# Seven products in place of eight in the up projections of a two-layer transformer kernel

## The chip, the cores and the metric

The kernel runs on one core of one Trainium2 chip. The metric is device time per execution in microseconds (us), the median of several runs, lower is better. Engines are called PE (matmul), DVE (vector), ACT (scalar), POOL and SP; here SP only issues DMAs.

## The reference

256 tokens of width 2048 pass two layers, each an attention mixer and an MLP. The change is in the MLP alone:

```python
h = rms_norm(x, norm_mlp[i])
x = x + jnp.square(jax.nn.relu(h @ w_up[i])) @ w_down[i]
```

`w_up[i]` is 2048 x 8192, `w_down[i]` 8192 x 2048, all in fp32.

## The kernel before

A weight matrix is worked through in **items**: 256 rows by 512 columns (512 KB). For each item a raw fp32 block is loaded by SP (`load`, L978), ACT rounds it to `wh` (L995) and DVE forms the rest `wl` (L996). PE multiplies high by high, low by high and high by low: 2 token halves x 2 row blocks x 3 = 12 matmuls of 128x512, `wh` first, `wl` in the last third (`high_first`). The items stand in one list. At item i the program splits item i+2 (`LEAD`) and loads item i+7 (five raw buffers, three pairs of `wh`, `wl`), runs item i's matmuls, then its `post` steps, then the steps that `later` set due. Instructions under `keep` hold this order on their engine; the sections on both sides of the MLPs are ordered by a scheduler.

The MLP goes in four slices f of 2048 hidden columns, in the order up(0), up(1), down(0), up(2), down(1), up(3), down(2), down(3). **Up** before: four chunks c of 512 columns, each of 8 items, summed in PSUM (`acc`). `up_done` hands a finished chunk to `to_features`: DVE transposes 32x32 blocks (L167), SP writes four pieces to DRAM (`td`, L173) an item later and reads them back (L179) four items after that, and `relu2` (DVE, L348), `high` (ACT, L353) and `low` (DVE, L358) make the two parts of `hT`, the left operand of down.

**Down** before takes two column blocks of 512 at once (`down_pair`). Of the 8 row blocks two (`SEVEN = (0, 2)`) and the two token halves form a 2x2 by 2x2 block product, which the scheme of Strassen in Winograd's form does with seven half items of 6 matmuls instead of four items of 12. The other six row blocks are plain. One pair is the order

```python
TURNS = "G0 H0 s1 G1 s3 H1 G2 s6 H2 s5 G3 s7 H3 s2 G4 H4 s4 G5 H5".split()
```

G and H are the plain items of the two columns, s1 to s7 the products. `s5`, `s6`, `s7` have no load: they split sums of weight blocks that DVE makes (`t1` to `t4`, L464 to L473, into X, Z, Y). Their left operands are sums of token blocks, made by `sums` into `S`. Products s1, s5, s6, s7 land in `aux` PSUM and are gathered in `E` by `p1` (ACT, L477), `p6`, `p5`, `p7` (DVE, L480 to L487); `into` (L494) and `add_residual` (L310) add the results to the residual.

Of the kernel before, what the change touches and what calls it, by code (L numbers as in the profile page):

```python
# [17 lines left out]
P = 128  # L18
# [43 lines left out]
def trunk(ctx, tc, x, x_t, gains_t, w_in_a, w_out_a, w_in_b, w_out_b, rel_bias, w_up, w_down, out):  # L62
# [23 lines left out]
    def copy(o, i, scale=1.0):  # L86
        pin(act.activation(o, i, AF.Copy, scale=scale))
# [67 lines left out]
    def later(n, f, *a):  # L155

        due[clock[0] + n].append(lambda: f(*a))

    def to_features(parts, place, then, wait=0):


        n = sum(part.shape[1] // P for part in parts)
        y = tmp.tile([P, 8, P], F32, name="jx", bufs=3)[:, :n, :]
        m = 0
        for part in parts:
            k = part.shape[1] // P
            dve.transpose(y[:, m:m + k, :].rearrange("p k f -> p (k f)"), part)  # L167
            m += k
        d = drp.tile([4, 32, n, 4, 32], F32, name=f"td{n}", bufs=4)

        def write():
            for a in range(4):
                keep(nc.sync.dma_start(d[:, :, :, a, :].rearrange("b j n i -> j n b i"),  # L173
                                       y[32 * a:32 * a + 32].rearrange("p n (b i) -> p n b i", b=4)))
            later(4, read)

        def read():
            z = place()
            keep(nc.sync.dma_start(z, d.rearrange("b j n a i -> (b j) n (a i)")))  # L179
# [148 lines left out]
    def mlp(l, next_col):  # L328
# [2 lines left out]

        def begin(pl):
            sec["pool"] = pl

        def stats():
# [4 lines left out]
        def up_done(f, c, acc):  # L340
            def parts(z):
                hT = sec[f][:, 4 * c:4 * c + 4].rearrange("p k i (t q) -> p i t k q", t=2)
                return z.rearrange("p (t k) q -> p t k q", t=2), hT[:, 0], hT[:, 1]

            def relu2(z):
                if c == 0:
                    sec[f] = sec["pool"].tile([P, KT, 2, S], F32R, name="hT", bufs=2)
                keep(dve.scalar_tensor_tensor(z, z, 0.0, z, op0=OP.max, op1=OP.mult))  # L348
                later(1, high, z)

            def high(z):
                r, h, l = parts(z)
                keep(act.activation(h, r, AF.Copy))  # L353
                later(1, low, z)
# [5 lines left out]
            to_features(acc, any_tile, relu2)  # L360

        def down_done(f, g, acc):
            if f < 3 or next_col is not None:
# [24 lines left out]
        def sums(f):  # L388

            h = sec[f]  # L390
            a, b = any_tile(), any_tile()
            a = a.rearrange("p (q j t) e -> p q j (t e)", q=2, j=KB)
            hi, lo = (h[:, 0:2 * STEP, i, :].rearrange("p (q j) s -> p q j s", q=2)[:, :, :KB]
                      for i in range(2))
            dve.tensor_add(a, hi.bitcast(F32), lo.bitcast(F32))
            b4 = b.rearrange("p (s j) e -> p s j e", s=4)
            (a11, a21), (a12, a22) = ((a[:, q, :, :P], a[:, q, :, P:]) for q in range(2))
            dve.tensor_add(b4[:, 0], a21, a22)
            dve.tensor_sub(b4[:, 1], b4[:, 0], a11)
            dve.tensor_sub(b4[:, 2], a11, a21)  # L400
            dve.tensor_sub(b4[:, 3], a12, b4[:, 1])
            z = sec["S"] = sec["pool"].tile([P, 2, 4 * KB, P], F32R, name="S", bufs=1)
            copy(z[:, 0], b)
            dve.tensor_sub(z[:, 1], b, z[:, 0].bitcast(F32))

        def down_pair(f, n):


            base = len(items)
            keys = [("dn", 2 * n + i) for i in range(2)]  # L410
            qs = [q for q in range(QB) if q not in SEVEN]

            def plain(col, i):
                def mm(wh, wl):
                    if i == 0:
                        acc = accp.tile([P, 2, 512], F32, name="acc")
                        accs[keys[col]] = [acc[:, t, :] for t in range(2)]
                    acc, L = accs[keys[col]], sec[f]
                    for t, j, part, wx, a, z in high_first(wh, wl):
                        keep(pe.matmul(acc[t], L[:, KB * qs[i] + j, part, t * P:(t + 1) * P],  # L420
                                       wx[:, j, :], start=a and i == 0,
                                       stop=z and i == len(qs) - 1))
                it = Item(rows(w_down[l], 2048 * f + KB * P * qs[i], KB * P,
                               1024 * n + 512 * col, 512), KB, 512, mm)
                if i == len(qs) - 1:
                    it.post.append(lambda: down_done(f, 2 * n + col, accs.pop(keys[col])))
                return it

            def seventh(left, src, to=None):


                def mm(wh, wl):
                    if to is None:
                        p = auxp.tile([P, 512], F32, name="aux")
                    else:
                        p = accs[keys[to[0]]][to[1]]
                    for t, j, part, wx, a, z in high_first(wh, wl, 1):
                        keep(pe.matmul(p, left(part, j), wx[:, j, :], start=to is None and a,  # L438
                                       stop=to is None and z))
                    it.product = p  # L440
                own_rows = not isinstance(src, str)
                it = Item(src if own_rows else None, KB, 512, mm)
                if not own_rows:
                    it.form = lambda: sec[src]
                return it

            def own(q, t):
                return lambda part, j: sec[f][:, KB * q + j, part, t * P:(t + 1) * P]

            def summed(i):  # L450
                return lambda part, j: sec["S"][:, part, KB * i + j, :]

            def block(col, q):
# [12 lines left out]
            def t2():
                keep(dve.tensor_sub(new("Z"), seven["s3"].raw, sec["X"]))

            def t3():
                keep(dve.tensor_sub(sec["Y"], seven["s3"].raw, sec["Y"]))  # L470
# [2 lines left out]
                keep(dve.tensor_sub(sec["Z"], seven["s2"].raw, sec["Z"]))  # L473

            def p1():
                sec["E"] = sec["pool"].tile([P, 4, 512], F32, name="E", bufs=1)
                keep(act.activation(sec["E"][:, 0], seven["s1"].product, AF.Copy))  # L477

            def p6():
# [9 lines left out]
                                    sec["E"][:, 1:3]))  # L489

            def into(t):
                xc = xs[:, t, 1024 * n:1024 * n + 1024].rearrange("p (c e) -> p c e", c=2)
                E = sec["E"].rearrange("p (c t) e -> p c t e", t=2)[:, :, t]
                keep(dve.scalar_tensor_tensor(xc, E, sec["rs2"][:, t:t + 1], xc,  # L494
                                              op0=OP.mult, op1=OP.add))

            qa, qb = SEVEN
            seven = {
# [11 lines left out]
            items[base - 8].early.append(load_y)  # L510
            for name, step in (("H0", t1), ("s1", p1), ("G1", t2), ("H1", t3), ("H2", p6), ("G3", p5),
                               ("H3", t4), ("G4", p7), ("H4", lambda: into(0)),
                               ("G5", lambda: into(1))):
                items[base + TURNS.index(name)].post.insert(0, step)

        def down(f):
            tail = next_col is None and f == 3
# [17 lines left out]
        items[10].post.append(stats)  # L535
        return items, begin


# [523 lines left out]
```

## Time and profile before

| | us |
|---|---|
| median of 3 runs (2063.6 to 2066.08) | 2064.94 |
| the profiled execution | 2063.33 |
| its span in the profile | 2061.5 |
| PE busy / DVE busy / ACT busy | 2053.8 / 1453.9 / 1025.4 |

The profile is of one execution; the chain that ended last runs through PE alone but for shares that round to nothing. PE's busy time counts 390 ns for a matmul that overlaps its neighbours, so the pace is read from the start times of the timeline.

### The profile page before, as it was taken

The page shows a single profiled execution, that of the slowest core. Times are in us where ns is not written, and L with a number is a line of the kernel's source. Part 1 is how long each engine was busy: PE and PEld are TensorE (multiplying, and loading weights), DVE is VectorE, ACT ScalarE, POOL GpSimd, SP SyncE. Part 2 cuts the span into 40 slices and gives each one's busy share as a digit, 9 for nine tenths or more (in the row PEclk, how much of TensorE's full clock was granted, in tenths as well). Part 3 has the DMA queues.
Part 4 walks back from the last instruction along what each step waited for, and adds up shares of the span by engine and source line. Part 5 has one row for each costly group of instructions (what it writes and reads, how often), then busy time and mean ns, then how long its engine had stood idle before and what let it go on. Part 6 is the DMA issues. An engine that isn't in the chain of part 4 may idle for free. (4 is left out here: it accounts for less than half of the span.)

```text
span 2061.5 us, 24939 instructions
## 1 busy us (share of the span) xinstructions
PE 2053.8 (100%) x9164; PEld 1697.1 (82%) x9164; DVE 1453.9 (71%) x1581; ACT 1025.4 (50%) x1233; POOL 28.9 (1%) x71
## 2 busy tenths in 40 slices
PE   9999999999999999999999999999999999999999
PEld 7888888888888888888887788888888888888887
DVE  5555655666687687678885798675668767867885
ACT  6555554544454454455554566454445445444543
POOL 0110100000000000000000000000000000000000
PEclk9999999999999999999999999999999999999999
DMA  9888856888866876876688688498886678678664
GB/s 315 236 228 213 237 173 202 264 240 247 238 220 184 246 242 194 234 229 213 192 253 251 195 251 259 150 255 245 247 257 213 196 234 243 192 211 259 205 196 164
DMA packets 477467, 464.85 MB, mean 225 GB/s; under 512 B 269664, under 2 KB 279968, under 8 KB 477344
## 3 DMA queue, kind: packets, MB, share of 16 engines
q1 hardware_dynamic: 469488, 455.81, 74.1%
q10 hardware_dynamic: 7856, 7.45, 1.3%
q8 instruction: 72, 1.18, 0.2%
q14 instruction: 51, 0.42, 0.1%
HBM read 425.90 MB, written 37.22 MB: 225 GB/s over the span
## 5 line engine op out<-in xcount | busy, mean ns | idle before, releaser
L996 DVE TENSOR_TENSOR wl<-wraw,wh 128x1024 fp32r<-128x1024 f32 (+1 forms) x725 | 881.6, 1218 | 481.0 <-ACT wh L995 466.2
L995 ACT ACTIVATE wh<-wraw 128x1024 fp32r<-128x1024 f32 (+1 forms) x725 | 765.3, 1057 | 820.2 <-PE acc L294 558.4
L294 PE MATMUL acc<-wh,xT 128*128 128x512 f32 x3264 | 811.8, 390 | 2.2 <-ACT xT L198 2.1
L294 PEld LDWEIGHTS acc<-wh,xT 128*128 128x128 f32 x3264 | 610.8, 188 | 130.5 <-ACT xT L198 2.3
L294 PE MATMUL acc<-wl,xT 128*128 128x512 f32 x1632 | 437.4, 390 | 0.0
L294 PEld LDWEIGHTS acc<-wl,xT 128*128 128x128 f32 x1632 | 306.2, 188 | 64.2 <-DVE wl L996 0.3
L420 PE MATMUL acc<-wh,hT 128*128 128x512 f32 x1440 | 355.7, 389 | 0.0
L420 PEld LDWEIGHTS acc<-wh,hT 128*128 128x128 f32 x1440 | 270.3, 188 | 56.2
L420 PE MATMUL acc<-wl,hT 128*128 128x512 f32 x720 | 192.5, 389 | 0.2 <-DVE wl L996 0.2
L420 PEld LDWEIGHTS acc<-wl,hT 128*128 128x128 f32 x720 | 135.1, 188 | 28.6 <-DVE wl L996 0.6
L294 PE MATMUL acc<-wh,oT 128*128 128x512 f32 x512 | 128.9, 391 | 0.0
L294 PEld LDWEIGHTS acc<-wh,oT 128*128 128x128 f32 x512 | 95.5, 188 | 19.8
L167 DVE STREAM_TRANSPOSE jx<-acc 128x512 f32<-128x512 f32 x68 | 44.7, 696 | 42.3 <-PE acc L294 39.7
L294 PE MATMUL acc<-wl,oT 128*128 128x512 f32 x256 | 69.4, 392 | 0.0
L294 PEld LDWEIGHTS acc<-wl,oT 128*128 128x128 f32 x256 | 47.8, 188 | 9.8
L995 ACT ACTIVATE wh<-Z 128x1024 fp32r<-128x1024 f32 x30 | 31.9, 1062 | 35.6 <-PE acc L438 24.3
L438 PE MATMUL aux<-wh,S 128*128 128x512 f32 x180 | 48.1, 389 | 0.0
L353 ACT ACTIVATE hT<-jx 128x1024 fp32r<-128x1024 f32 x32 | 34.0, 1062 | 27.9 <-DVE jx L348 27.9
L996 DVE TENSOR_TENSOR wl<-Z,wh 128x1024 fp32r<-128x1024 f32 x30 | 36.7, 1225 | 5.3 <-ACT wh L995 3.8
L438 PEld LDWEIGHTS aux<-wh,S 128*128 128x128 f32 x180 | 33.8, 188 | 7.0
L310 DVE SCALAR_TENSOR_TENSOR xs<-acc,rs,xs 128x512 f32<-128x512 f32 x56 | 39.4, 743 | 0.0
L358 DVE TENSOR_TENSOR hT<-jx,hT 128x1024 fp32r<-128x1024 f32 x32 | 39.0, 1218 | 0.0
(191 smaller groups left out, 1237.2 us busy)
## 6 DMA issues: line engine op xcount, KB each, us to landing
wraw<-in_w_up_dram SPq DMA_DIRECT2D x256, 512.0 KB, 4.5
wraw<-in_w_down_dram SPq DMA_DIRECT2D x241, 512.0 KB, 4.7
wraw<-in_w_in_a_dram SPq DMA_DIRECT2D x94, 512.0 KB, 4.6
wraw<-in_w_in_b_dram SPq DMA_DIRECT2D x64, 512.0 KB, 4.7
td<-jx SPq DMA_DIRECT2D x240, 128.0 KB, 4.4
jx<-td SPq DMA_DIRECT2D x45, 512.0 KB, 6.5
wraw<-in_w_out_a_dram SPq DMA_DIRECT2D x32, 512.0 KB, 4.0
wraw<-in_w_out_b_dram SPq DMA_DIRECT2D x32, 512.0 KB, 4.7
```

The source lines that it names most:

```text
L167: dve.transpose(y[:, m:m + k, :].rearrange("p k f -> p (k f)"), part)
L294: (keep if alone else pin)(pe.matmul(acc[t], L[:, KB * q + j, part, t * P:(t + 1) * P], wx[:, j, :], start=a and q == 0, stop=z and q == ( ...
L310: dve.scalar_tensor_tensor(xc, acc[t], scale[:, t:t + 1], xc, op0=OP.mult, op1=OP.add)
L353: keep(act.activation(h, r, AF.Copy))
L358: keep(dve.tensor_sub(l, r, h.bitcast(F32)))
L420: keep(pe.matmul(acc[t], L[:, KB * qs[i] + j, part, t * P:(t + 1) * P], wx[:, j, :], start=a and i == 0, stop=z and i == len(qs) - 1))
L438: keep(pe.matmul(p, left(part, j), wx[:, j, :], start=to is None and a, stop=to is None and z))
L995: order(act.activation(wh[:, a], raw[:, a], AF.Copy))
L996: order(dve.tensor_sub(wl[:, a], raw[:, a], wh[:, a].bitcast(F32)))
```

## The change

Up now goes by pairs as well: `pair` is the old `down_pair` with the left operand and the weights as arguments. Slice 0's first two chunks stay as they were (`up_classical`), the other 14 column pairs of the two layers run 19 entries of `TURNS` instead of 16 items. `sums` is cut into four steps spread over items and is also called on `xT`, the left operand of up. A pair's result is whole only in `E`: `gather` adds the plain sum from PSUM, the transposition reads `E` (128x1024 at once), and the writes, reads and the steps on the chunk are set on named turns of the next pair. Relu and square are two ACT instructions instead of one on DVE. The diff, cut:

```diff
         def begin(pl):
             sec["pool"] = pl
+            for name, shape, dt in (("S", [P, 2, 4 * KB, P], F32R), ("E", [P, 4, 512], F32),
+                                    *((n, [P, KB, 512], F32) for n in "XYZ")):
+                sec[name] = pl.tile(shape, dt, name=name, bufs=1)
...
-            def relu2(z):
+            def relu(z):
                 if c == 0:
                     sec[f] = sec["pool"].tile([P, KT, 2, S], F32R, name="hT", bufs=2)
-                keep(dve.scalar_tensor_tensor(z, z, 0.0, z, op0=OP.max, op1=OP.mult))
-                later(1, high, z)
+                keep(act.activation(z, z, AF.Relu))
+
+            def square(z):
+                keep(act.activation(z, z, AF.Square))
...
-        def up(f):
-            for c, q in side_by_side(4, QB, 2 if f == 0 else 1):
+        def up_classical(f):
+            for c, q in side_by_side(2, QB):
                 tokens_out(items, ("up", c), w_up[l], 0, 2048 * f + 512 * c, lambda: xT, q,
                            lambda acc, c=c: up_done(f, c, acc), alone=True)
...
+            def gather(col):
+                E = sec["E"][:, 2 * col:2 * col + 2]
+                keep(dve.tensor_add(E, accs.pop(keys[col]), E))
+
+            turning = {}
+
+            def turn_chunk(col):
+                turning[col] = turned([sec["E"][:, 2 * col:2 * col + 2].rearrange("p t e -> p (t e)")])
...
+            at(spot("G5"), gather, 0)
+            at(spot("H5"), turn_chunk, 0)
+            at(spot("G0", 1), gather, 1)
+            at(spot("s1", 1), turn_chunk, 1)
+            for col, places in enumerate((("G0", "H1"), ("G1", "H2"))):
+                at(spot(places[0], 1), write, col)
+                at(spot(places[1], 1), read, col)
+                relu, square, high, low = inner(chunk[0], 2 * chunk[1] + col)
+                rest = (("G3", "H3", "G4"), ("G4", "H4", "G5"))[col]
+                for name, step in zip(rest, (relu, square, high)):
+                    at(spot(name, 1), lambda step=step, col=col: step(turning[col]))
+                at(late[col](spot), lambda low=low, col=col: low(turning[col]))
+
+        def up(f, n, last):
+            pair(w_up[l], 0, 2048 * f + 1024 * n, lambda: xT, chunk=(f, n),
+                 late=(lambda spot: spot("G0", 2), lambda spot: spot("G2", 2)) if last else
+                 (lambda spot: spot("H4", 1), lambda spot: spot("s1", 2)))
...
-        up(0)
+        up_classical(0)
+        sums(lambda: xT, (11, 12, 13, 14))
+        up(0, 1, False)
         for f in range(3):
-            up(f + 1)
-            items[-20].post.append(lambda f=f: sums(f))
+            up(f + 1, 0, False)
+            up(f + 1, 1, True)
+            then_sums(lambda f=f: sec[f], ("H2", "s2", "H4", "G5"))
             down(f)
-        items[-4].post.append(lambda: sums(3))
+            then_sums((lambda: xT) if f < 2 else (lambda: sec[3]), ("H2", "s2", "H4", "H5"))
         down(3)
```

The order changes as follows. First DVE, of the kernel before, from the end of down(0) through the first chunk of up(2) (`L310` adds to the residual, `L395` to `L400` are the first of `sums`):

```order
L310 SCALAR_TENSOR_TENSOR xs<-acc,rs_3294,xs 128x512 x2
L996 TENSOR_TENSOR wl<-wraw,wh 128x1024 x8
L167 STREAM_TRANSPOSE jx<-acc 128x512 x2
L395 TENSOR_TENSOR jx<-hT 128x1024
L996 TENSOR_TENSOR wl<-wraw,wh 128x1024
L398 TENSOR_TENSOR jx<-jx 128x256
L400 TENSOR_TENSOR jx<-jx 128x256
```

Now DVE of the changed kernel, from the end of the pair up(1, 0) into up(1, 1). L1088 is the split, L533 `gather`, L380 `low`; L498, L501 and L504 are `t1` to `t3`:

```order
L533 TENSOR_TENSOR E<-acc,E 128x1024
L1088 TENSOR_TENSOR wl<-wraw,wh 128x1024
L498 TENSOR_TENSOR X<-Y,wraw 128x1024
L1088 TENSOR_TENSOR wl<-wraw,wh 128x1024
L380 TENSOR_TENSOR hT<-jx,hT 128x2x4x128
L167 STREAM_TRANSPOSE jx<-E 128x1024
L1088 TENSOR_TENSOR wl<-wraw,wh 128x1024
L501 TENSOR_TENSOR Z<-wraw,X 128x1024
L1088 TENSOR_TENSOR wl<-wraw,wh 128x1024
L1088 TENSOR_TENSOR wl<-Z,wh 128x1024
L504 TENSOR_TENSOR Y<-wraw,Y 128x1024
```

Where eight splits followed one another, other instructions of 1024 columns now stand between almost any two.

ACT of the changed kernel in the pair behind up(1, 1), from the split for s4 to that for the next pair's G0 (L1087 is the split, L369 Relu, L372 Square, L376 `high`):

```order
L1087 ACTIVATE wh<-Z 128x1024
L376 ACTIVATE hT<-jx 128x2x4x128
L369 ACTIVATE jx<-jx 128x1024
L1087 ACTIVATE wh<-wraw 128x1024
L372 ACTIVATE jx<-jx 128x1024
L1087 ACTIVATE wh<-wraw 128x1024 x2
L376 ACTIVATE hT<-jx 128x2x4x128
```

The six steps on two chunks stand within eight consecutive turns, Relu of the second chunk right behind `high` of the first; before, a chunk left ACT the one step `high` (L353).

SP of the changed kernel at the first pair of layer 0, up(0, 1), and the next (`td_3406`, `td_3428` are the two chunks of `up_classical`, `td_3757` and `td_3814` those of the pair):

```order
L175 DMA td_3406<-jx 256x4x32 x4
L175 DMA td_3428<-jx 256x4x32 x4
L1070 DMA wraw<-in_w_up_dram 128x2x512 x2
L180 DMA jx<-td_3406 128x1024
L1070 DMA wraw<-in_w_up_dram 128x2x512
L180 DMA jx<-td_3428 128x1024
L1070 DMA wraw<-in_w_up_dram 128x2x512 x5
L495 DMA Y<-in_w_up_dram 128x2x512
L1070 DMA wraw<-in_w_up_dram 128x2x512 x7
L175 DMA td_3757<-jx 256x4x32 x4
L1070 DMA wraw<-in_w_up_dram 128x2x512 x2
L175 DMA td_3814<-jx 256x4x32 x4
```

Eight chunk writes stand in one run at the first pair; in every later pair two weight loads stand between two groups of four.

## Rows read from the trace of the kernel before

**Rows 1.** The page's busy time of each engine: us, share of the span, instructions.

```profile
PE 2053.8 (100%) x9164; PEld 1697.1 (82%) x9164; DVE 1453.9 (71%) x1581; ACT 1025.4 (50%) x1233; POOL 28.9 (1%) x71
```

**Rows 2.** Busy time by stretch: from:to, length, busy us (instructions) of PE, PEld, DVE, ACT, POOL, granted clock, DMA share, GB/s. In order: the start, an up stage, two halves of down(0), the entry into the second mixer, the second mixer, the end.

```profile
0.00:40.00 40.00, 38.02 (x157) 30.38 (x158) 22.53 (x29) 26.50 (x45) 1.09 (x8) 1.00 0.96 339
...
480.00:520.00 40.00, 40.00 (x178) 33.13 (x177) 26.73 (x28) 18.80 (x18) 0.00 (x0) 1.00 0.80 245
...
560.00:600.00 40.00, 40.00 (x178) 33.14 (x177) 36.40 (x34) 22.11 (x22) 0.00 (x0) 1.00 0.73 226
600.00:640.00 40.00, 40.00 (x178) 33.10 (x178) 32.51 (x31) 19.78 (x20) 0.00 (x0) 1.00 0.59 185
...
1080.00:1120.00 40.00, 37.92 (x173) 30.83 (x173) 22.93 (x33) 16.94 (x24) 0.00 (x0) 1.00 0.86 245
...
1160.00:1200.00 40.00, 40.00 (x188) 31.80 (x187) 37.64 (x97) 22.94 (x44) 0.00 (x0) 1.00 0.72 192
...
2040.00:2080.00 40.00, 18.12 (x86) 15.07 (x84) 9.44 (x12) 4.72 (x5) 0.00 (x0) 0.99 0.09 28
```

**Rows 3.** PE's timeline in down(0) and, last, in up(1): start us, us, engine, line, operation, tiles, how many in a row.

```profile
563.09 1.07 PE L438 MATMUL aux<-wh,hT 128*128 128x512 f32 x4
564.00 0.61 PE L438 MATMUL aux<-wl,hT 128*128 128x512 f32 x2
564.45 1.98 PE L420 MATMUL acc<-wh,hT 128*128 128x512 f32 x8
566.26 1.07 PE L420 MATMUL acc<-wl,hT 128*128 128x512 f32 x4
567.17 1.07 PE L438 MATMUL acc<-wh,S 128*128 128x512 f32 x4
...
489.65 1.98 PE L294 MATMUL acc<-wh,xT 128*128 128x512 f32 x8
491.46 1.07 PE L294 MATMUL acc<-wl,xT 128*128 128x512 f32 x4
492.37 1.98 PE L294 MATMUL acc<-wh,xT 128*128 128x512 f32 x8
```

**Rows 4.** Groups of DVE instructions: busy us, mean ns of one | idle us just before them, and what ended it.

```profile
L996 DVE TENSOR_TENSOR wl<-wraw,wh 128x1024 fp32r<-128x1024 f32 x719 | 877.2, 1222 | 476.6 <-ACT wh L995 463.3 <-PE acc L294 8.5 <-issue 1.7
L167 DVE STREAM_TRANSPOSE jx<-acc 128x512 f32<-128x512 f32 x68 | 44.7, 696 | 42.3 <-PE acc L294 39.7 <-DMA wraw<-in_w_up_dram 2.6
...
L348 DVE SCALAR_TENSOR_TENSOR jx<-jx 128x1024 f32<-128x1024 f32 x32 | 38.8, 1213 | 0.0
L494 DVE SCALAR_TENSOR_TENSOR xs<-E,rs,xs 128x1024 f32<-128x1024 f32 x30 | 38.4, 1279 | 0.0
...
L487 DVE TENSOR_TENSOR E<-aux,E 128x1024 f32<-128x1024 f32 x15 | 18.3, 1218 | 0.0
...
L483 DVE TENSOR_TENSOR E<-aux,E 128x512 f32<-128x512 f32 x15 | 10.3, 684 | 0.0
...
L395 DVE TENSOR_TENSOR jx<-hT 128x1024 f32<-128x1024 f32 x8 | 9.5, 1192 | 0.0
...
L398 DVE TENSOR_TENSOR jx<-jx 128x256 f32<-128x256 f32 x8 | 3.4, 420 | 1.4 <-DMA td<-jx 1.4
```

**Rows 5.** DVE's timeline at the start of down(0): start us, us, then as above.

```profile
560.19 1.21 DVE L348 SCALAR_TENSOR_TENSOR jx<-jx 128x1024 f32<-128x1024 f32 x1
561.32 1.22 DVE L996 TENSOR_TENSOR wl<-wraw,wh 128x1024 fp32r<-128x1024 f32 x1
562.46 1.22 DVE L464 TENSOR_TENSOR X<-Y,wraw 128x1024 f32<-128x1024 f32 x1
563.59 1.22 DVE L996 TENSOR_TENSOR wl<-wraw,wh 128x1024 fp32r<-128x1024 f32 x1
```

**Rows 6.** Groups of ACT instructions, columns as in rows 4.

```profile
L353 ACT ACTIVATE hT<-jx 128x1024 fp32r<-128x1024 f32 x32 | 34.0, 1062 | 27.9 <-DVE jx L348 27.9
...
L477 ACT ACTIVATE E<-aux 128x512 f32<-128x512 f32 x15 | 9.0, 599 | 17.8 <-PE aux L438 17.8
```

**Rows 7.** Timelines of SP, ACT and PE at the last pair of layer 0's down(3), where two chunks are transposed for the next mixer.

```profile
1030.07 7.27 SPq L173 DMA_DIRECT2D td<-jx  x8
1037.44 1.16 SPq L978 DMA_DIRECT2D wraw<-in_w_down_dram  x2
...
1042.65 1.06 ACT L995 ACTIVATE wh<-wraw 128x1024 fp32r<-128x1024 f32 x1 [3.68 <-DMA wraw<-in_w_down_dram]
...
1051.33 1.07 PE L438 MATMUL aux<-wh,S 128*128 128x512 f32 x4
1052.45 0.73 PE L438 MATMUL aux<-wl,S 128*128 128x512 f32 x2
1053.02 2.00 PE L420 MATMUL acc<-wh,hT 128*128 128x512 f32 x8
1055.17 1.19 PE L420 MATMUL acc<-wl,hT 128*128 128x512 f32 x4 [0.16 <-DVE wl L996]
1056.20 1.08 PE L438 MATMUL acc<-wh,hT 128*128 128x512 f32 x4
```

**Rows 8.** DMA issues: count, KB each, median us from issue to landing.

```profile
wraw<-in_w_up_dram SPq DMA_DIRECT2D x256, 512.0 KB, 4.5
...
td<-jx SPq DMA_DIRECT2D x240, 128.0 KB, 4.4
jx<-td SPq DMA_DIRECT2D x45, 512.0 KB, 6.5
```

More of the change, by code (lines that the diff above doesn't have):

```diff
@@ L157, in later, with turned @@
         due[clock[0] + n].append(lambda: f(*a))
-    def to_features(parts, place, then, wait=0):
+    def turned(parts):
         n = sum(part.shape[1] // P for part in parts)
@@ L166, in to_features, with turned_out, turned_in, read @@
             k = part.shape[1] // P
-            dve.transpose(y[:, m:m + k, :].rearrange("p k f -> p (k f)"), part)
+            (keep if n == 8 and k == 8 else lambda ins: None)(
+                dve.transpose(y[:, m:m + k, :].rearrange("p k f -> p (k f)"), part))
             m += k
+        return y
+    def turned_out(y):
+        n = y.shape[1]
         d = drp.tile([4, 32, n, 4, 32], F32, name=f"td{n}", bufs=4)
-        def write():
[L172 to L177, printed above, removed]
+        for a in range(4):
+            keep(nc.sync.dma_start(d[:, :, :, a, :].rearrange("b j n i -> j n b i"),
+                                   y[32 * a:32 * a + 32].rearrange("p n (b i) -> p n b i", b=4)))
+        return d
+    def turned_in(z, d):
+        keep(nc.sync.dma_start(z, d.rearrange("b j n a i -> (b j) n (a i)")))
+    def to_features(parts, place, then, wait=0):
+        y = turned(parts)
+        def write():
+            later(4, read, turned_out(y))
+        def read(d):
             z = place()
-            keep(nc.sync.dma_start(z, d.rearrange("b j n a i -> (b j) n (a i)")))
+            turned_in(z, d)
             if then is not None:
@@ L358, in low, with up_done, then @@
                 keep(dve.tensor_sub(l, r, h.bitcast(F32)))
-            to_features(acc, any_tile, relu2)
+            return relu, square, high, low
+        def up_done(f, c, acc):
+            def then(z):
+                for n, step in enumerate(inner(f, c)):
+                    if n:
+                        later(n, step, z)
+                    else:
+                        step(z)
+            to_features(acc, any_tile, then)
         def down_done(f, g, acc):
@@ L406, in down_pair, with sums, whole, four @@
-        def down_pair(f, n):
+        def sums(src, where):
+            def whole():
+                h, a = src(), sec["X"].rearrange("p q (j s) -> p q j s", j=KB)
+                hi, lo = (h[:, 0:2 * STEP, i, :].rearrange("p (q j) s -> p q j s", q=2)[:, :, :KB]
+                          for i in range(2))
+                keep(dve.tensor_add(a, hi.bitcast(F32), lo.bitcast(F32)))
+            def four():
+                a = sec["X"].rearrange("p q (j s) -> p q j s", j=KB)
+                b = sec["sums"] = any_tile()
+                b = b.rearrange("p (s j) e -> p s j e", s=4)
+                (a11, a21), (a12, a22) = ((a[:, q, :, :P], a[:, q, :, P:]) for q in range(2))
+                keep(dve.tensor_add(b[:, 0], a21, a22))
+                keep(dve.tensor_sub(b[:, 1], b[:, 0], a11))
+                keep(dve.tensor_sub(b[:, 2], a11, a21))
+                keep(dve.tensor_sub(b[:, 3], a12, b[:, 1]))
+            def high():
+                keep(act.activation(sec["S"][:, 0], sec["sums"], AF.Copy))
+            def low():
+                z = sec["S"]
+                keep(dve.tensor_sub(z[:, 1], sec["sums"], z[:, 0].bitcast(F32)))
+            for i, step in zip(where, (whole, four, high, low)):
+                at(i, step)
@@ L409, in down_pair, with pair @@
+        def pair(w, r0, c0, left, done=None, chunk=None, late=None):
             base = len(items)
-            keys = [("dn", 2 * n + i) for i in range(2)]
+            keys = [("pair", base + i) for i in range(2)]
             qs = [q for q in range(QB) if q not in SEVEN]
@@ L415, in mm, with seventh @@
                     if i == 0:
-                        acc = accp.tile([P, 2, 512], F32, name="acc")
-                        accs[keys[col]] = [acc[:, t, :] for t in range(2)]
-                    acc, L = accs[keys[col]], sec[f]
+                        accs[keys[col]] = accp.tile([P, 2, 512], F32, name="acc")
+                    acc, L = accs[keys[col]], left()
                     for t, j, part, wx, a, z in high_first(wh, wl):
-                        keep(pe.matmul(acc[t], L[:, KB * qs[i] + j, part, t * P:(t + 1) * P],
+                        keep(pe.matmul(acc[:, t, :], L[:, KB * qs[i] + j, part, t * P:(t + 1) * P],
                                        wx[:, j, :], start=a and i == 0,
                                        stop=z and i == len(qs) - 1))
[L423 to L429, printed above, removed]
+                return Item(block(col, qs[i]), KB, 512, mm)
+            def seventh(lhs, src, to=None):
                 def mm(wh, wl):
@@ L435, in mm @@
                     else:
-                        p = accs[keys[to[0]]][to[1]]
+                        p = accs[keys[to[0]]][:, to[1], :]
                     for t, j, part, wx, a, z in high_first(wh, wl, 1):
-                        keep(pe.matmul(p, left(part, j), wx[:, j, :], start=to is None and a,
+                        keep(pe.matmul(p, lhs(part, j), wx[:, j, :], start=to is None and a,
                                        stop=to is None and z))
@@ L491, in into @@
             def into(t):
+                n = chunk
                 xc = xs[:, t, 1024 * n:1024 * n + 1024].rearrange("p (c e) -> p c e", c=2)
@@ L510, in down_pair, with spot, finish @@
             items[base - 8].early.append(load_y)
+            def spot(name, turns=0):
+                return base + TURNS.index(name) + turns * len(TURNS)
             for name, step in (("H0", t1), ("s1", p1), ("G1", t2), ("H1", t3), ("H2", p6), ("G3", p5),
-                               ("H3", t4), ("G4", p7), ("H4", lambda: into(0)),
-                               ("G5", lambda: into(1))):
-                items[base + TURNS.index(name)].post.insert(0, step)
+                               ("H3", t4), ("G4", p7)):
+                at(spot(name), step)
+            if done is not None:
+                at(spot("H4"), into, 0)
+                at(spot("G5"), into, 1)
+                for col in range(2):
+                    def finish(col=col):
+                        acc = accs.pop(keys[col])
+                        done(2 * chunk + col, [acc[:, t, :] for t in range(2)])
+                    at(spot("GH"[col] + "5"), finish)
+                return
+            at(spot("G5"), gather, 0)
[14 more added lines that the diff above has]
+                 (lambda spot: spot("H4", 1), lambda spot: spot("s1", 2)))
+        def down_pair(f, n):
+            pair(w_down[l], 2048 * f, 1024 * n, lambda: sec[f],
+                 lambda g, acc: down_done(f, g, acc), n)
         def down(f):
@@ L534, in mlp @@
             items[-2].post.append(add_early)
-        items[10].post.append(stats)
+        at(10, stats)
+        for i in sorted(hooks):
+            items[i].post += hooks[i]
         return items, begin
```

44 lines of the change are left out of this document (17 added, 27 removed).

## The prediction

> **What bounds the kernel now.** I read the page's busy times first: PE is busy 2053.8 of 2061.5 us, DVE 71% and ACT 50% of the span [rows 1]. Then the busy times by stretch, to see where PE loses the 7.7 us that are missing: 2.0 in the first 40 us, 2.1 at the entry into the second mixer, 3.4 at the end (18.1 of the last 21.5 us) and next to nothing elsewhere [rows 2]. In the MLPs PE is full both where DVE works 26.7 us of 40 (up) and where it works 36.4 of 40 (down, which already uses the seven products), at a granted clock of 1.00 of full speed [rows 2]. So the time of an MLP is its number of matmuls times their pace, as long as splits arrive. The pace is in PE's timeline: a plain item of 12 matmuls takes 2.72 us from start to start (564.45 to 567.17), in up as in down (489.65 to 492.37), and a product item of 6 takes 1.36 (563.09 to 564.45) [rows 3]; both are 0.2267 us a matmul. A product costs PE nothing beyond its matmuls.
>
> **What the change removes on PE.** A column pair of up was 16 plain items, 16 x 2.72 = 43.52 us. Now it is 12 plain items and 7 products, 12 x 2.72 + 7 x 1.36 = 42.16 us. That is 6 matmuls and 1.36 us less in each of 14 pairs: **19.04 us**, all of it on the engine that sets the end. This part is arithmetic; the rest is whether DVE, ACT and SP keep up in 42.16 us a pair.
>
> **DVE, per new pair.** A 1024-wide operation is recorded at about 1.22 us [rows 4], but back to back such operations start every 1.13 to 1.14 us (560.19, 561.32, 562.46, 563.59) [rows 5]; I use 1.135. A pair has 19 splits, four weight sums, `p7`, two `gather`, two transpositions and two `low`: 30 wide operations, 34.1 us. `gather` adds PSUM to SBUF as `p7` does (1.218), with 1.279 of `into` as the upper bound [rows 4]. A transposition of 1024 is not in the trace: 0.696 is one of 512, two are 1.39 and no more; adding the 512 columns at the step between `p5` and `p7`, 1.218 - 0.684 = 0.53, gives 1.23 [rows 4], which I take, 0.1 above a slot, so 0.2 a pair. `p6` and `p5` at 0.684 less the same overlap are 1.2. Together 35.5 us. The four steps of `sums` add 1.1 + 4 x 0.34 + 1.135 = 3.6 (0.420 recorded for a small one, less the same overlap) [rows 4], now in 12 of the kernel's 29 pairs. So DVE needs **35.5 us, or 39.1 with sums, of 42.16**: 84 and 93%. The nearest stretches are 36.40 of 40 (91%) and 37.64 of 40 (94%), and PE was full in both [rows 2]. What leaves DVE is `relu2`, 1.213 a chunk, and two transpositions from PSUM.
>
> **ACT, per new pair.** 19 splits, `p1`, and two chunks of Relu, Square and `high`. Relu and Square at this shape are not in the trace; the nearest is the copy `high` of the same shape at 1.062 [rows 6], and I take that for both. Bounds: the cheapest form of 512 columns, 0.599 [rows 6], and twice that, 1.2. The sum is 25 x 1.06 + 0.6 = 27.1 us, 64% of the pair, 28.2 with the rounding of S. It hides beside PE: `wh` of item i+2 may be written once PE has read `wh` of item i-1, a third of an item and two items before it is needed, at least 0.45 + 1.36 + 2.72 = 4.5 us for 1.06 us of work. In the densest turns (H3 to G5) four steps on chunks go between the splits, and that cover shrinks to about 2 us but stays.
>
> The Trainium skill, "ScalarE: Activation LUTs", Rules for kernel authors, says to put relu, max and mul on VectorE, not on ScalarE. Here one pass costs 1.062 on ACT and 1.213 on DVE [rows 4, 6], so the trace disagrees per pass in fp32; by the rule DVE would keep 2.3 us a pair and stand at 41.4 of 42.16 with sums, and PE's sum would be the same.
>
> **Waits that the change adds.** On DVE, `gather` waits for the last matmul of its column, with the splits of the next turns queued behind it; PE waits for those only two items later. The earlier kernel had its transpositions from PSUM at the same place (39.7 us of DVE idle on PE in all) [rows 4], with PE full. On ACT, `p1` waits for the transposition of E, and Relu for the chunk's read, 6.5 us after its issue [rows 8]; it is issued at H1 and used at G3, five turns or 10.9 us later. `wh` splits are queued behind both. On SP, four chunk writes wait for the transposition and hold back weight loads behind them: eight writes took 7.27 us to issue, so four take 3.6 [rows 7]; a load lands 4.5 us after its issue [rows 8] and its split comes five turns later, 5 x 42.16 / 19 = 11.1 us. Behind four writes it still lands in time (8.1), behind eight it doesn't (11.8). The number of chunk writes, reads and weight bytes is unchanged. Up to here the loss is nothing.
>
> One place of the trace shows a loss. In the last pair of layer 0's down(3) two chunks are written in one run of eight, the weight load behind them is late, ACT waits 3.68 us for it, and the backlog reaches PE: s7 takes 1053.02 - 1051.33 = 1.69 instead of 1.36, and H3 3.18 (to 1056.20) instead of 2.72 [rows 7]. That is **0.79 us**. The first new pair of each layer has the same run of eight writes, the same two loads behind it, and the same pair of chunks on ACT and DVE. I charge it 0.79, so 1.58 for two layers, and the other 12 pairs nothing, since they have two loads between the groups of four. The bounds: nothing anywhere, or 0.79 in each of the 14 pairs, 11.1.
>
> **The sum.** The profiled execution took 2063.33 (span 2061.5 and 1.8 around it). 2063.33 - 19.04 + 1.58 = 2045.87; the median stands 1.61 above that execution, so I forecast **2047.5**. Both mixers, the start and the end keep their order.
>
> **The rivals.**
> - *Late loads in every new pair.* Every pair writes two chunks while it loads weights at four fifths and more of the DMA share [rows 2]. For it: the one place where this met a full DVE lost time [rows 7]. Against it: there the writes stood in one run. It gives 2064.94 - 19.04 + 11.06 = 2057.0, still faster.
> - *The chunks come late to ACT.* If Relu stands waiting for its read as that split waited for its load, and each of 28 chunks costs PE 0.79, the loss is 22.1 and the time 2068.0, no change. Against it: 10.9 us between issue and use for a landing of 6.5.
> - *DVE becomes the bound* in the 12 pairs with sums, and the kernel slower. By the recorded durations without overlap such a pair is 30 x 1.22 + 0.02 + 1.37 + 1.19 + 4 x 0.42 + 1.22 = 42.1 us; with the 2.36 us that DVE idled in its fullest stretch [rows 2] 44.5, which is 2.3 above PE's 42.16. If nothing of it is carried by the prefetch, 12 x 2.3 = 27.6 and 2064.94 - 19.04 + 27.6 = 2073.5. It decides for slower from 1.93 us lost a pair ((19.04 + 4.13) / 12). Against it: starts 1.135 apart [rows 5], and the lighter pairs between, which win it back.
>
> The Trainium skill, "VectorE: DVE Perf Modes", The DRAIN you can't avoid, would bring this about: it says that the next operation does not start until the pipeline has emptied, so 1.22 per operation. The trace disagrees: starts 1.135 apart at 1.22 each [rows 5].
>
> That the change saves no matmuls is excluded: the built order has 84 fewer on PE.
>
> **How the numbers follow.** Forecast 0.73, late loads 0.14, late chunks 0.06, DVE the bound 0.05, 0.02 for anything else. 0.2% (4.13 us) is about what a measurement of this kernel can tell from no change. Forecast and late loads are faster, late chunks are the same: faster 0.87, same 0.07, slower 0.06. The range goes from no loss at all, 2045.9, less the 1.3 by which the fastest run lies under the median, 2044.5, to the late loads, 2057.0.
>
> **What would show it.** After: PE still 100% busy, with 84 fewer matmuls, span near 2044; product items in up at 1.36 and plain ones at 2.72; DVE about 36 to 39 us in 42 in the up stages, ACT about 27. Lengthened s7, H3 or G4 items in the first pair of each layer are my 0.79; the same in every pair are the first rival. ACT idle before Relu on the chunk's read, longer than 2 us, is the second. PE idle on `wl` at the pairs with sums, with DVE busy without a gap, is the third. The forecast is wrong if the span loses less than 14 us.

## The result and the profile after

The changed kernel takes **2044.79 us** (median of 4 runs, 2044.66 to 2045.54); the kernel before took 2064.71 beside it (4 runs, 2063.6 to 2066.08). The ratio is 0.9903, 95% interval 0.9891 to 0.9914. Forecast were 2047.5 and a range of 2044.5 to 2057.0. The profiled execution took 2044.88, its span is 2043.2, so 18.45 below the profiled execution before.

The page's busy time of each engine, as in [rows 1]:

```profile
PE 2035.1 (100%) x9080; PEld 1681.2 (82%) x9080; DVE 1608.0 (79%) x1725; ACT 1138.6 (56%) x1359; POOL 29.2 (1%) x71
```

84 matmuls fewer, DVE 154 us and ACT 113 us busier, and PE still busy 8 us less than the span. By stretch, columns as in [rows 2]: two new pairs from one `t1` to the next, without and with sums (the first two rows), then the last pair of layer 0's down(3), and the first new pair of layer 1:

```profile
473.24:515.40 42.16, 42.16 (x187) 34.91 (x186) 35.30 (x33) 26.25 (x26) 0.00 (x0) 1.00 0.86 251
515.40:557.56 42.16, 42.16 (x187) 34.91 (x186) 38.59 (x38) 27.09 (x27) 0.00 (x0) 1.00 0.80 245
...
1040.00:1080.00 40.00, 39.30 (x172) 31.88 (x171) 33.36 (x46) 19.66 (x28) 0.00 (x0) 1.00 0.81 235
1400.00:1440.00 40.00, 39.73 (x175) 32.12 (x174) 30.80 (x30) 23.11 (x24) 0.00 (x0) 1.00 0.75 217
```

A pair lasts 42.16 us with PE full, DVE busy 35.30 or 38.59 of it and ACT 26.25 or 27.09. Only in the last two rows PE lacks something. PE's timeline in up(1), as in [rows 3], shows a product item and a plain one:

```profile
474.40 1.07 PE L476 MATMUL aux<-wh,xT 128*128 128x512 f32 x4
...
475.76 1.98 PE L462 MATMUL acc<-wh,xT 128*128 128x512 f32 x8
...
478.48 1.07 PE L476 MATMUL acc<-wh,S 128*128 128x512 f32 x4
```

1.36 us (474.40 to 475.76) and 2.72 (to 478.48), in up as in down. The new groups, as in [rows 4, 6]: busy us, mean ns of one | idle before, and what ended it:

```profile
L369 ACT ACTIVATE jx<-jx 128x1024 f32<-128x1024 f32 x32 | 33.5, 1046 | 2.2 <-DMA jx<-td 2.2
L372 ACT ACTIVATE jx<-jx 128x1024 f32<-128x1024 f32 x32 | 33.4, 1045 | 0.0
...
L167 DVE STREAM_TRANSPOSE jx<-E 128x1024 f32<-128x1024 f32 x28 | 34.6, 1236 | 0.0
L533 DVE TENSOR_TENSOR E<-acc,E 128x1024 f32<-128x1024 f32 x28 | 34.1, 1218 | 10.0 <-PE acc L462 10.0
```

Relu and Square take 1.046 and 1.045, the transposition 1.236, `gather` 1.218. Relu waited for its read only 2.2 us in all 32 chunks, and DVE 10.0 us for PE before `gather`; neither reached PE outside the first new pair of layer 1. That place, as in [rows 7], SP, ACT and PE:

```profile
1406.32 7.12 SPq L175 DMA_DIRECT2D td<-jx  x8
1413.54 1.15 SPq L1070 DMA_DIRECT2D wraw<-in_w_up_dram  x2
...
1418.43 1.06 ACT L1087 ACTIVATE wh<-wraw 128x1024 fp32r<-128x1024 f32 x1 [1.48 <-DMA wraw<-in_w_up_dram]
...
1422.55 1.06 ACT L369 ACTIVATE jx<-jx 128x1024 f32<-128x1024 f32 x1 [1.04 <-DMA jx<-td]
...
1430.22 0.61 PE L476 MATMUL aux<-wl,S 128*128 128x512 f32 x2
1430.94 2.14 PE L462 MATMUL acc<-wh,xT 128*128 128x512 f32 x8
...
1433.84 1.07 PE L476 MATMUL acc<-wh,xT 128*128 128x512 f32 x4
1435.07 0.73 PE L476 MATMUL acc<-wl,xT 128*128 128x512 f32 x2 [0.17 <-DVE wl L1088]
1435.63 1.54 PE L462 MATMUL acc<-wh,xT 128*128 128x512 f32 x6
```

Eight chunk writes in one run, a load and a chunk read late for ACT, then the backlog at s7, H3 and s2: 1430.22 to 1435.63 is 5.41 us for 20 matmuls, which at full pace are 20 x 0.2267 = 4.53.

**Where the time went.** PE's start times cut the execution at the first item of each MLP and, for the second mixer, at its first matmul behind the last one of layer 0's MLP. Layer 0's MLP lasts 678.15 us where it was 687.19, layer 1's (to the end of the last matmul) 678.44 where it was 687.03. Seven pairs should save 7 x 1.36 = 9.52 each. In layer 1 the difference is 8.59: 0.93 less. In layer 0 it is 9.04: 0.48 less, since s7 and H3 in the last pair of down(3), whose turns the change leaves in their order, now lose 1.30 (1041.52 to 1046.90 for 18 matmuls of 0.2267) where they lost 0.79. ACT and PE there:

```profile
1033.36 1.06 ACT L1087 ACTIVATE wh<-wraw 128x1024 fp32r<-128x1024 f32 x1 [4.21 <-DMA wraw<-in_w_down_dram]
...
1041.52 1.07 PE L476 MATMUL aux<-wh,S 128*128 128x512 f32 x4
1043.15 0.72 PE L476 MATMUL aux<-wl,S 128*128 128x512 f32 x2 [0.56 <-DVE wl L1088]
...
1046.90 1.08 PE L476 MATMUL acc<-wh,hT 128*128 128x512 f32 x4
```

The run of eight writes takes 7.60 us there and ACT waits 4.21 us for the load behind it, for 7.27 and 3.68 before [rows 7]. This is not the scatter of one profile of the changed kernel: in the profiles of all ten experiments the writes take 7.78 to 8.03 us and ACT waits 4.11 to 4.49. Why the writes take longer is not shown. The time ahead of layer 0's MLP and the second mixer are 0.29 and 0.44 shorter. The sum, -9.04 - 8.59 - 0.29 - 0.44 = -18.36, is the span's difference (18.3). The medians differ by 19.92, more than the 19.04 of the removed matmuls although some of it was lost again; the account above is of the two profiled executions.

### The profile page after: what moved, and what is told of

Its sections match the earlier page's. It is cut to its first block, busy times and chain, and to the rows that moved or that the text cites. A ratio compares the mean times of both kernels' runs of the same rounds, so it can differ in the third digit from the quotient of the medians.

```text
span 2043.2 us, 25135 instructions
## 1 busy us (share of the span) xinstructions
PE 2035.1 (100%) x9080; PEld 1681.2 (82%) x9080; DVE 1608.0 (79%) x1725; ACT 1138.6 (56%) x1359; POOL 29.2 (1%) x71
## 3 DMA queue, kind: packets, MB, share of 16 engines
q8 instruction: 71, 1.16, 0.2%
## 5 line engine op out<-in xcount | busy, mean ns | idle before, releaser
L1088 DVE TENSOR_TENSOR wl<-wraw,wh 128x1024 fp32r<-128x1024 f32 (+1 forms) x711 | 862.4, 1216 | 324.8 <-ACT wh L1087 306.6
L1087 ACT ACTIVATE wh<-wraw 128x1024 fp32r<-128x1024 f32 (+1 forms) x711 | 750.1, 1056 | 630.1 <-PE acc L306 243.3
L306 PE MATMUL acc<-wh,xT 128*128 128x512 f32 x1472 | 369.1, 391 | 1.5 <-ACT xT L210 1.5
L462 PE MATMUL acc<-wh,xT 128*128 128x512 f32 x1344 | 332.1, 389 | 0.1
L306 PEld LDWEIGHTS acc<-wh,xT 128*128 128x128 f32 x1472 | 274.6, 188 | 59.6 <-ACT xT L210 1.8
L462 PEld LDWEIGHTS acc<-wh,xT 128*128 128x128 f32 x1344 | 252.2, 188 | 52.9 <-ACT wh L1087 0.5
L306 PE MATMUL acc<-wl,xT 128*128 128x512 f32 x736 | 197.9, 390 | 0.0
L462 PE MATMUL acc<-wl,xT 128*128 128x512 f32 x672 | 179.6, 389 | 0.0
L306 PEld LDWEIGHTS acc<-wl,xT 128*128 128x128 f32 x736 | 138.0, 188 | 29.2 <-DVE wl L1088 0.3
L462 PEld LDWEIGHTS acc<-wl,xT 128*128 128x128 f32 x672 | 126.1, 188 | 26.3
L1087 ACT ACTIVATE wh<-Z 128x1024 fp32r<-128x1024 f32 x58 | 61.6, 1062 | 75.1 <-PE acc L476 45.7
L476 PE MATMUL aux<-wh,S 128*128 128x512 f32 x348 | 93.0, 389 | 0.0
L1088 DVE TENSOR_TENSOR wl<-Z,wh 128x1024 fp32r<-128x1024 f32 x58 | 71.0, 1224 | 11.5 <-ACT wh L1087 9.2
L476 PEld LDWEIGHTS aux<-wh,S 128*128 128x128 f32 x348 | 65.3, 188 | 13.6
```

The source lines that it names most:

```text
L306: (keep if alone else pin)(pe.matmul(acc[t], L[:, KB * q + j, part, t * P:(t + 1) * P], wx[:, j, :], start=a and q == 0, stop=z and q == ( ...
L462: keep(pe.matmul(acc[:, t, :], L[:, KB * qs[i] + j, part, t * P:(t + 1) * P], wx[:, j, :], start=a and i == 0, stop=z and i == len(qs) - 1))
L476: keep(pe.matmul(p, lhs(part, j), wx[:, j, :], start=to is None and a, stop=to is None and z))
L1087: order(act.activation(wh[:, a], raw[:, a], AF.Copy))
L1088: order(dve.tensor_sub(wl[:, a], raw[:, a], wh[:, a].bitcast(F32)))
```

## The experiments

"After" is the changed kernel, 2044.79; every ratio is to the kernel before. Layer durations are cut as above.

**Relu squared back on DVE**

```diff
-                keep(act.activation(z, z, AF.Relu))
+                keep(dve.scalar_tensor_tensor(z, z, 0.0, z, op0=OP.max, op1=OP.mult))
...
-                keep(act.activation(z, z, AF.Square))
+                pass
```

> Relu squared goes back to DVE as one instruction at Relu's place; ACT's Square step is empty; all else as in the changed kernel. Theory (PE sets the end, DVE at 1.135 us a wide operation has room): DVE rises from 35.5 to 37.8 us a new pair, 41.4 with sums, of PE's 42.16, ACT falls by 4.2 us a pair. Time 2044.8 to 2047, so at most 2 us more, lost at single crowded turns. Rival (an operation occupies DVE for its recorded 1.22 us, so DVE is at its limit in pairs with sums): 6 of the 14 new pairs have sums and would need 44.5 us, 2.4 more than PE: about 14 us more, 2059.

Measured: 2044.57 (2043.48 to 2045.16), ratio 0.9897 [0.988, 0.9913]. The same two pairs as above, with PE as full:

```profile
473.24:515.40 42.16, 42.16 (x188) 34.91 (x187) 37.28 (x34) 22.57 (x22) 0.00 (x0) 1.00 0.84 250
515.40:557.56 42.16, 42.16 (x188) 34.91 (x187) 40.67 (x40) 23.54 (x23) 0.00 (x0) 1.00 0.80 243
```

DVE works 40.67 of 42.16 us and nothing is lost: the time is just under the range of the theory and far from the rival's 2059. The move of Relu to ACT is worth nothing in time here, and DVE has room up to that. Layer 1's MLP took 677.51 us, which is 687.03 - 9.52; with ACT relieved the 0.93 is gone.

**The seven products in layer 0's up alone**

The diff, cut (the sums of xT are left out in layer 1 as well):

```diff
         def up(f, n, last):
+            if l == 1:
+                for c in (2 * n, 2 * n + 1):
+                    for q in range(QB):
+                        tokens_out(items, ("up", c), w_up[l], 0, 2048 * f + 512 * c, lambda: xT, q,
+                                   lambda acc, c=c: up_done(f, c, acc), alone=True)
+                return
...
```

> Seven products in up only in layer 0; layer 1's up projections are plain items in pairs of chunks. Theory (each new pair saves its 6 matmuls, 1.36 us, wherever it stands): 7 of 14 pairs, so 9.52 us more than the changed kernel, less the about 0.9 us that layer 1's first new pair lost: 2053.4 to 2054.3. Rival (the gain comes from one layer, or from the new order of sums and tiles rather than the matmuls): either near 2045 or near 2064.

Measured: 2054.28 (2053.98 to 2054.9), ratio 0.9945 [0.9931, 0.996]. Layer 1's MLP lasts 687.03 us, as in the kernel before, layer 0's 678.15, as after. The gain belongs to the pairs and adds up by layer.

**Four and eight more wide DVE operations a pair** (`t1`, `t2` and both `low`, shown for `t1`; the second kernel has 3)

```diff
-                keep(dve.tensor_sub(sec["X"], sec["Y"], seven["s1"].raw))
+                for _ in range(1 if done is not None else 2):
+                    keep(dve.tensor_sub(sec["X"], sec["Y"], seven["s1"].raw))
```

> In each new pair t1, t2 and the two low steps run twice on the same operands: four wide DVE operations more, 4.54 us at 1.135, so 40.0 us a pair and 43.6 with sums, of 42.16. Theory (PE sets the end; DVE wide operations start 1.135 apart): pairs without sums stay hidden; the 6 with sums are 1.4 us over, at most 8.6 us in all and less if the prefetch of two items carries part: 2045 to 2053.5. Rival (recorded 1.22 us each): 44.1 and 46.9 us, so 8 x 1.9 + 6 x 4.7 = 43 us: 2088.

Measured: 2046.99 (2045.71 to 2047.47), ratio 0.9909 [0.9894, 0.9923], 2.2 over after, which is within what the two intervals leave open. In the profile PE waits for `wl` in one pair with sums of each layer, 0.51 us, and loses 0.78 at each of these places.

> The same steps run three times: eight wide DVE operations more, 9.08 us, so 44.6 us a pair and 48.1 with sums, of PE's 42.16. Theory: DVE now sets the end in the up projections: 8 x 2.4 + 6 x 6.0 = 55 us over PE, less a few us of prefetch at each change between up and down: 2085 to 2100, PE waiting on wl. Rival (1.22 us each): 49.0 and 51.8 us, 8 x 6.8 + 6 x 9.6 = 112 us: 2157. Second rival (DVE has more room than its count says): under 2060.

Measured: 2088.84 (2086.31 to 2089.98), ratio 1.0111 [1.0095, 1.0126]: 44 over after and slower than the kernel before. DVE and PE in a pair with sums, and the stretch:

```profile
518.28 3.74 DVE L500 TENSOR_TENSOR X<-Y,wraw 128x1024 f32<-128x1024 f32 x3
521.93 1.22 DVE L1091 TENSOR_TENSOR wl<-wraw,wh 128x1024 fp32r<-128x1024 f32 x1
...
523.82 1.98 PE L463 MATMUL acc<-wh,xT 128*128 128x512 f32 x8
529.12 2.07 PE L463 MATMUL acc<-wl,xT 128*128 128x512 f32 x4 [3.32 <-DVE wl L1091]
```

```profile
515.40:560.00 44.60, 40.84 (x173) 33.02 (x172) 44.22 (x43) 25.33 (x26) 0.00 (x0) 0.96 0.72 212
```

DVE is busy 44.22 of 44.60 us and PE waits for `wl`. So the third rival exists: it shows first at four extra operations a pair, and makes the kernel slower than the one before between four and eight. Durations of 1.22 each would have given 2088 for the first kernel and 2157 for the second; both times lie in the range written for the theory. The doses were larger than written, though: three runs of `t1` take 3.65 us from start to start (518.28 to 521.93), so a repeat costs (3.65 - 1.14) / 2 = 1.26, not 1.135. The pairs are then at 35.3 + 4 x 1.26 = 40.3 and, with sums, 43.6 with four; 45.4 and 48.7 with eight. Four lose 2.2 of at most 6 x 1.5 = 9, eight lose 44 of at most 8 x 3.2 + 6 x 6.5 = 65. In the profile some 28 us of the 44 are waits of PE in the MLPs, and behind some of them the matmuls ran at a granted clock of 0.50 to 0.63. That the prefetch and the lighter pairs of down carry the rest is my reading; no run shows it by itself.

**The two plain chunks two items apart**

```diff
-            for c, q in side_by_side(2, QB):
+            for c, q in side_by_side(2, QB, 2, 2):
```

> The two plain chunks ahead of the first new pair end two items apart instead of one after the other, so their eight chunk writes no longer stand in one run on SP (four, a weight load, four). Theory (the about 0.9 us that PE loses in layer 1's first new pair, s7 to s2, come from the run of eight writes: the weight load behind it is late, and the two chunks' steps then crowd on ACT): that loss goes, layer 0 is unchanged, time 2043.9. Rival (the writes are not it, the chunks' steps on ACT are): the loss stays, 2044.8.

Measured: 2044.81 (2043.85 to 2046.13), ratio 0.99 [0.9885, 0.9915]. That is the number of the rival, but the 0.9 between the two is less than the runs of this kernel scatter, so the time decides nothing. In the profile the theory holds. The timeline at the place of the loss:

```profile
1407.17 0.64 SPq L1070 DMA_DIRECT2D wraw<-in_w_up_dram  x1
1407.91 4.61 SPq L175 DMA_DIRECT2D td<-jx  x4
...
1418.47 1.07 ACT L1087 ACTIVATE wh<-wraw 128x1024 fp32r<-128x1024 f32 x1 [0.82 <-PE acc L462]
1419.43 1.05 ACT L369 ACTIVATE jx<-jx 128x1024 f32<-128x1024 f32 x1
...
1430.91 0.62 PE L476 MATMUL aux<-wl,S 128*128 128x512 f32 x2
1431.37 1.98 PE L462 MATMUL acc<-wh,xT 128*128 128x512 f32 x8
```

The split waits for PE, no longer for a load; Relu waits for nothing; s7 ends in time, and layer 1's MLP takes 677.51. The kernel with Relu on DVE reached the same 677.51 with the run of eight left in place and ACT waiting 1.86 us for the load behind it: the 0.93 needs both, late loads and a full ACT. In layer 0 of the changed kernel the eight writes also stand in one run, but there ACT waits for no load and only 0.58 us for a chunk.

**The reads of the chunks four or five turns late**

```diff
-            for col, places in enumerate((("G0", "H1"), ("G1", "H2"))):
+            for col, places in enumerate((("G0", "s5"), ("G1", "s2"))):
```

> In each new pair the two chunks are read back four and five turns later than in the changed kernel (at s5 and s2 instead of H1 and H2), one turn ahead of Relu, so that a read that lands 6.5 us after its issue comes some 3 to 4 us after ACT could start Relu. This makes the late chunks of the second rival happen on purpose, 28 times. By that rival's price, 0.79 us a chunk: 22 us, 2067. If ACT's splits are two items ahead of PE and carry about 2 us of such a wait: the rest, 1 to 2 us a chunk, comes through, 28 to 56 us, 2073 to 2100. If the cover carries it all: 2045.

Measured: 2093.43 (2086.54 to 2098.56), ratio 1.0132 [1.0111, 1.0154]. ACT and PE at one chunk, and the stretches before and behind the wait:

```profile
551.22 1.06 ACT L369 ACTIVATE jx<-jx 128x1024 f32<-128x1024 f32 x1 [5.59 <-DMA jx<-td]
...
548.86 0.61 PE L476 MATMUL acc<-wl,xT 128*128 128x512 f32 x2
553.28 3.69 PE L462 MATMUL acc<-wh,xT 128*128 128x512 f32 x8 [3.80 <-ACT wh L1087]
556.80 1.08 PE L462 MATMUL acc<-wl,xT 128*128 128x512 f32 x4
```

```profile
549.30:553.20 3.90, 0.17 (x1) 0.00 (x0) 0.00 (x0) 1.98 (x3) 0.00 (x0) 1.00 0.27 103
553.20:557.00 3.80, 3.72 (x9) 3.02 (x10) 3.26 (x3) 3.80 (x6) 0.00 (x0) 0.55 0.34 98
```

ACT waits 5.59 us, PE 3.80, and the eight matmuls behind the wait take 3.52 us (553.28 to 556.80) instead of 1.81, at a granted clock of 0.55. The loss is (2093.43 - 2044.79) / 28 = 1.7 us a chunk on average, within the second case expected; the forecast's rival had 0.79. The dose is not the rival's, though: ACT waits up to 5.64 us for a read here, and the 0.79 came from a wait of 3.68. In the profiled execution, the slowest of the four, PE waits once in each of the 14 pairs, 34.4 us in all, of the 54.0 that the two MLPs lose; behind seven of these waits the granted clock was between 0.50 and 0.66, which makes most of the rest. So the second rival was a real danger, avoided by where the reads stand.

**The seven products in layer 0's first chunks too**

The diff, cut (the load of Y and `t1` of this pair also move to where the first items allow them):

```diff
...
-        up_classical(0)
-        sums(lambda: xT, (11, 12, 13, 14))
+        if l == 0:
+            sums(lambda: xT, (0, 0, 0, 1))
+            up(0, 0, False)
+        else:
+            up_classical(0)
+            sums(lambda: xT, (11, 12, 13, 14))
```

> In layer 0 the first two chunks of up(0) also go by the seven products (15 of 16 pairs; the sums of xT stand on the first two items of the MLP). Theory (6 matmuls less on PE wherever splits arrive): 1.36 us less, 2043.4. Rival (at the MLP's first items xT, its sums, or Y come too late, and PE or DVE waits there): PE idle at the start of the MLP, no gain or some us lost, 2045 to 2050.

Measured: 2051.15 (2049.05 to 2051.71), ratio 0.9928 [0.9915, 0.994]: 6.4 over after, the rival's way and a little beyond its range. ACT and PE at the start of the MLP, and the stretches before, in and behind the wait:

```profile
391.66 1.06 ACT L440 ACTIVATE S<-jx 128x1024 fp32r<-128x1024 f32 x1 [3.76 <-DVE jx L437]
...
390.56 0.61 PE L476 MATMUL aux<-wl,xT 128*128 128x512 f32 x2
395.31 3.78 PE L462 MATMUL acc<-wh,xT 128*128 128x512 f32 x8 [4.14 <-ACT wh L1091]
398.89 1.83 PE L462 MATMUL acc<-wl,xT 128*128 128x512 f32 x4
```

```profile
380.00:390.50 10.50, 10.50 (x48) 8.71 (x47) 7.22 (x14) 3.75 (x8) 0.00 (x0) 1.00 0.84 242
390.50:395.30 4.80, 0.68 (x3) 0.21 (x2) 1.37 (x7) 3.64 (x7) 0.00 (x0) 0.83 0.20 32
395.30:399.00 3.70, 3.69 (x9) 2.92 (x10) 3.70 (x6) 2.33 (x3) 0.00 (x0) 0.50 0.33 89
```

The split for G1 stands behind the rounding of S, which waits for DVE's sums of xT; PE waits 4.14 us and then runs at 0.50.

**The same, with the two plain chunks of layer 1 two items apart** (this edit and that of the chunks apart together)

> Both: 15 pairs in all (16 of layer 0's chunks by the seven products), and in layer 1 the two plain chunks two items apart. If both theories hold the gains add: 1.36 + 0.9 us less than the changed kernel, 2042.5. If only one holds, 2043.4 or 2043.9.

Measured: 2049.73 (2049.59 to 2050.41), ratio 0.9924 [0.9911, 0.9936]. Of the two theories only the one on layer 1 holds: layer 0 loses the same 4.14 us in a wait; layer 1's MLP is at 677.51 again.

**The same, with the sums' steps later** (the places 0, 0, 2, 2 and 0, 1, 2, 2 instead of 0, 0, 0, 1)

> As the kernel with 15 pairs and the plain chunks of layer 1 two items apart, but the rounding of the sums S at the start of layer 0's MLP stands two items later on ACT, behind the splits of G1 and s3 instead of ahead of them. Theory (what cost the 15-pair kernels 4.1 us of PE's wait and the slow items behind it was the split of G1 queued on ACT behind the rounding of S, which waited 3.76 us for DVE): that wait goes, S comes about when s3 needs it, and the time is 2042.5 to 2044. Rival (S cannot be ready at the fifth item wherever its steps stand, so PE now waits for S instead): PE idle before s3 by 1 to 4 us, 2045 to 2050.

> The same with the four small sums on DVE one item later as well, behind one more split. Theory: as the kernel before it in this batch, 2042.5 to 2044, if S is in time; by the rival S comes at most about 1.2 us (one split on DVE) later than there, and PE waits that much more before s3.

Measured: 2047.93 (2047.38 to 2049.78), ratio 0.9918 [0.9904, 0.9932], and 2047.45 (2046.47 to 2048.21), ratio 0.9913 [0.9899, 0.9927]. PE in the first of them:

```profile
393.20 0.39 PE L476 MATMUL acc<-wh,S 128*128 128x512 f32 x1
396.11 0.97 PE L476 MATMUL acc<-wh,S 128*128 128x512 f32 x3 [2.52 <-DVE S L444]
...
1086.57 3.08 PE L306 MATMUL acc<-wh,xT 128*128 128x512 f32 x9 [1.91 <-ACT xT L210]
```

The first time is in the rival's range and the second no later. G1 is in time, and PE now waits 2.52 us for S itself (2.33 in the second kernel, so the later small sums didn't lengthen the wait). That is more than the 1.36 which the pair saves: layer 0's MLP lasts 679.78 and 679.93 us, for 678.37 in the kernel that has only the chunks apart. The other part of the excess stands elsewhere: in the profiled executions the second mixer is 1.8 and 2.0 us longer than in that kernel. Behind waits of 1.91 and 2.11 us at its entry (the last line above) the granted clock was 0.65 up to 1091.0, while the kernel with the chunks apart kept 1.00 behind 1.75 us there, and the kernel before behind 2.08. None of the three placements tried lets the first pair pay; none of these kernels beats the changed one.

## Why the prediction was right

- **The main term, 19.04 us, was right.** Undisturbed, a layer saves exactly 9.52 (687.03 to 677.51 for layer 1 in five experiments), and a layer without the change keeps its old duration.
- **DVE, 35.5 and 39.1 us a pair, was right**: 35.30 and 38.59. The transposition, not in the trace before, was taken at 1.23; it is 1.236 recorded, and starts 1.16 apart. The Trainium skill, "VectorE: DVE Perf Modes", The DRAIN you can't avoid, has each operation wait until the pipeline of the last is empty, and adds that one which is not held starts earlier. The trace of after shows the latter, as that of before did, for operations that need nothing of the one directly ahead (1.14 apart at 1.22 recorded). The repeats, which write the same tile again, start 1.26 apart.
- **ACT, 27.1 and 28.2, was right**: 26.25 and 27.09. Relu and Square came out at 1.046 and 1.045 for 1.06 assumed.
- **The Trainium skill's rule to keep relu on VectorE** ("ScalarE: Activation LUTs", Rules for kernel authors; its reason there is a rate in bf16, and all is fp32 here): no difference in the time, 2044.57 against 2044.79, since both engines hide it beside PE. In the one crowded place the rule's side was the better one, by the 0.93.
- **The charge of 0.79 for the first new pair of each layer was half right.** Layer 0's lost nothing, though its eight writes stand in one run as well; layer 1's lost 0.93. A further 0.51 came where no term stood, in down(3), and came in every experiment. That these are 1.44 in all, for 1.58, is luck.
- **The start and the mixer** were taken as unchanged and came out 0.73 shorter. That is within the scatter: in the other profiles layer 0's MLP starts between 383.39 and 385.15 us (383.28 in after) and the second mixer lasts 299.13 to 302.01.
- **The step from the profiled execution to the median, 1.61, failed.** The profiled execution of before lay under the four runs beside the changed kernel (2063.33 for 2063.6 and more); that of after lay 0.09 above its median. This is most of the 2.7 us between forecast and result: 1.70 here, and the 0.99 between 2045.87 and 2044.88, of which the two points above give 0.14 and 0.73. The result stands 0.3 above the range's lower end, and under 2045.9, where the forecast put a change without any loss.
- **The rivals.** Late loads in every pair: not seen. Late chunks: not seen; made on purpose they cost 1.7 us a chunk instead of 0.79, with longer waits than the forecast's, and with matmuls slowed behind half of PE's waits. DVE as the bound: not reached; it makes the kernel slower from between four and eight more operations a pair. Its margin is narrow: at 40.67 of 42.16 nothing was lost (relu squared on DVE), at 43.6 PE began to wait.

## What to carry to other kernels

Where one engine is full, count its instructions at their pace in place, and what goes off it is gained to the hundredth, so long as the other engines stay under it pair by pair. The danger is then in the order on the helpers' queues: an instruction that waits (a rounding of sums, a chunk that is read late) holds the bound engine's next operand behind it, and can cost more than the whole change brings at that place. And take a forecast's level from the median of several runs against the same in the next kernel, not from how one profiled execution stands in them.

## What had not been expected of the hardware

A wait of PE can cost more than its length. In the kernel with 15 pairs PE ran at a granted clock of 1.00 up to 390.50, was idle for 4.14 us, and in the next 3.70 us the clock was 0.50, which is the lower of its two levels, 1.2 GHz: eight matmuls took 3.58 us (395.31 to 398.89 in PE's timeline) for 1.81. With that the 15th pair, meant to save 1.36, lost layer 0 5.50 us (683.65 against 678.15). Not every wait does this, and its length alone does not decide: in the kernel with late reads the granted clock was 1.00 in the 3.4 us behind a wait of 3.02 us (at 776.64) and 0.66 in the 3.5 us behind one of 2.50 (at 1603.47). What decides, no run here shows.

On DVE an instruction that reads what the one directly ahead of it has written starts later. In the changed kernel the four small sums:

```profile
541.21 0.42 DVE L434 TENSOR_TENSOR jx<-X 128x256 f32<-128x256 f32 x1
541.66 0.43 DVE L435 TENSOR_TENSOR jx<-jx,X 128x256 f32<-128x256 f32 x1
542.01 0.42 DVE L436 TENSOR_TENSOR jx<-X 128x256 f32<-128x256 f32 x1
542.34 0.42 DVE L437 TENSOR_TENSOR jx<-X,jx 128x256 f32<-128x256 f32 x1
```

L435 needs L434's sum and starts 0.45 behind it; L436 and L437 need nothing of the one directly ahead and start 0.35 and 0.33 behind it. The repeats above, which write the same tile again, show the same: 1.26 against 1.135. All four sums stood at 0.34 in the forecast, 0.1 us too little in a pair with sums.
